# A conv-gated FFN on one core: seven half-sized products in place of eight in the up projection, activations through DRAM, and the down projection in one accumulation

## The chip, the cores and the metric

The kernel runs on one core of a Trainium2 chip. The metric is the device time of one execution in microseconds (us), and the number given for a kernel is the median of its runs.

## The reference, cut to what matters

Two transformer-like blocks follow one another on 1024 tokens of 1024 features in float32: a short-convolution layer, a stick-breaking attention layer, and a second block with two kinds of attention and a feed-forward part. The change is in the feed-forward part, which is the last thing that is computed before the final norm:

```python
D_MODEL = 1024; SEQ = 1024; D_FF = 2816; CONV_WIDTH = 3

def _conv_ffn(h, w_up, conv_w, conv_b, w_down):
    u = h @ w_up                                   # [1024, 1024] @ [1024, 5632]
    a, g = jnp.split(u, 2, axis=-1)
    s = a.shape[1]
    ap = jnp.pad(a, ((0, 0), (CONV_WIDTH - 1, 0), (0, 0)))
    a = ap[:, 0:s] * conv_w[0] + ap[:, 1:s + 1] * conv_w[1] + ap[:, 2:s + 2] * conv_w[2] + conv_b
    return (jax.nn.gelu(a, approximate=False) * g) @ w_down   # [1024, 2816] @ [2816, 1024]
...
        h2 = _rmsnorm(x, norm2_g[l]) * (1.0 + scale2) + shift2
        x = x + gate2 * _conv_ffn(h2, w_up[l], conv_w[l], conv_b[l], w_down[l])
    return _rmsnorm(x, final_g)
```

## The kernel before, in words

Activations lie feature-major: 128 features on the partitions, 512 tokens (a half) along the free dimension. Every float32 product is made of three matmuls on a rounded type: the weights are split into a high part `wh` (a cast by ScalarE) and a low part `wl` (a subtraction by VectorE), the activations likewise into the two halves of a tile `act`. For each 128x128 block of weights the function `proj` issues wh x high, wh x low and wl x high into one PSUM bank; a job with eight such blocks (eight k-tiles) is 24 matmuls of 512 columns. All matmuls of this kind are called `pj` in the profile.

Weights come as pieces of up to four k-tiles (256 KB). The list `stream` holds them in the order of use; `advance` issues the loads (SyncE's queue, SP) five pieces ahead of the use, the high parts three ahead and the low parts two ahead (eight, five and four in the last projection).

The instructions of all engines are put in order when the program is built. The class `Sched` keeps a rough clock for every engine. The projections drive; everything else is a side task, a generator that yields what it waits for and goes on once the clock of TensorE has passed that time. `until` runs side tasks until a condition holds. So the order on each engine is fixed, and on the chip an engine waits only where its next instruction isn't ready.

There are 34 large tiles (4 KB a partition) and 32 small ones (2 KB). `room` makes a side task wait until a large tile can be had.

The feed-forward part takes the 22 blocks of 128 features of `a` and of `g` in three groups (8, 7 and 7). For each group, `ups` makes the jobs `job_up` (all eight k-tiles, then the convolution, gelu and the gate in `post`, and the split of the result into an `act` tile that stays on chip), and `downs` makes the eight jobs of the down projection over the k-tiles of that group; its partial result is added to the residual and goes to DRAM (`x5_d`) and back. The first group runs half by half; in the rest (`lagged`) the second half of the tokens follows two jobs behind the first, with the same weights. The last group's second half runs in two passes of 256 tokens, so that the final norm of one can be done beside the other.

Before that, in block 2, the jobs `c1` make queries, keys and values of the second half of the tokens, attention of the second half runs as side tasks, `br` and `wo` are the output projections of each half, and `g1` are gate projections. `consume_ffn` makes the feed-forward input `h2` of the second half, `h2_side` that of the first.

Of the kernel before, what the change touches and what calls it, by code (L numbers as in the profile page):

```python
# [16 lines left out]
D = 1024  # L17
# [4 lines left out]
NF = DFF // 128  # L22
EPS = 1e-6
# [24 lines left out]
N_C = 2  # jobs before the first output of block 2  # L48
N_U = 2  # jobs kept for after the second branches
# [170 lines left out]
class Engine:  # L220
    """An engine whose instructions are noted by the scheduler."""
# [24 lines left out]
def tile_net(tc, *aps, **kw):  # L246
    """Emitted once into a context of its own, to learn when each tile is used last, then into tc."""
# [9 lines left out]
def tile_body(  # L257
# [95 lines left out]
    def advance(n):  # L353
        """Pieces up to n are about to be used."""
# [10 lines left out]
    def split_pieces(n):  # L365
        """Side task: the parts of the first pieces, as they arrive."""
# [79 lines left out]
    def proj_tok(pieces, name, half, b, ps, c0):  # L446
        """[128 tokens, 256 features] of token block b of a half: activations stationary."""
# [14 lines left out]
    def lagged(jobs, lag):  # L462
        """Jobs (pieces, fn(half, pieces)): the second half of the tokens runs lag jobs behind."""
# [12 lines left out]
    def staged(jobs, half):  # L476
        """All the jobs at once, each in a bank of its own, in stages of two k-tiles."""
# [46 lines left out]
    def load_vectors(items, tag, q):  # L524
        """1-D vectors as columns [128, n / 128]."""
# [37 lines left out]
    def gemv_add(acc, wt, sc, k, first=False):  # L563
        """The rows of k-tile k, weighed, summed over k-tiles only."""
# [5 lines left out]
    def sums(acc, turned):  # L570
        """Sums over the partitions of a [128, 512] tile, as columns: element p of each 128 on partition p."""
# [40 lines left out]
    def rstd_of(v, width):  # L612
        """v ** -0.5 on a narrow tile: square root, reciprocal, a Newton step."""
# [15 lines left out]
    def spread(r):  # L629
        """[128 tokens, 4] -> [128, 512], the same on every partition."""  # L630
# [11 lines left out]
    def rstd_rows(acc, n):  # L642
        """Squares, still to be summed over the partitions -> r of 512 tokens on every partition."""
# [8 lines left out]
    def norm_apply(xt, rb, gs, sh, key):  # L652
        """(x * gs) * r + sh, split."""
# [24 lines left out]
    x5_d = [scratch(f"x5_d{i}", [8, 128, S]) for i in range(2)]  # L678
# [8 lines left out]
    # ======================= block 1, convolution layer =======================  # L687
# [63 lines left out]
    def res_jobs(w, name, gate, x_dram, out_dram, done=None, extra_g=None, k0=0, nk=8, squares=True, pairs=False):  # L751
# [37 lines left out]
        def job(j):  # L789
# [8 lines left out]
            return chunk(w, j * 128, nk=nk, k0=k0), fn  # L798
# [5 lines left out]
    def norm_side(consume):  # L804
        """After the residual of a half: r for its tokens, then consume(r)."""
# [6 lines left out]
    def each(xs, gen, gap=1.25):  # L812
        """A task per tile, started one after the other."""
# [1019 lines left out]
```

## Time and profile before

| what | value |
|---|---|
| median of 3 runs | 2653.97 us (2653.41 to 2655.66) |
| span of the profiled execution, first to last instruction | 2650.7 us |
| time of the profiled execution itself | not listed beside its span; the median of the runs is 3.3 us above the span |
| TensorE busy | 2613.5 us (99%) |
| VectorE, ScalarE, GpSimd busy | 1635.7 us (62%), 1154.7 us (44%), 171.4 us (6%) |
| moved by DMA | 430.66 MB, 162 GB/s over the span |

The busy time of TensorE (PE) counts from an instruction's start to its modelled end, and those overlap; the distance from start to start is what a matmul costs. PEld are weight loads, which overlap the matmuls. DVE is VectorE, ACT ScalarE, POOL GpSimd; L241 and L242 are the lines of the helper through which all instructions are issued, so groups are told apart by the names of their tiles.

### The profile page before, as it was taken

The numbers are of one execution on the slowest core, as the hardware profiler recorded it, in microseconds if no ns is written. First come the engines' busy times: TensorE is split into PE (matmuls) and PEld (weight loads), VectorE is DVE, ScalarE is ACT, GpSimd is POOL, SyncE is SP. The second block draws the span as 40 slices with busy tenths as digits, with TensorE's granted clock in tenths as the row PEclk, the third lists the DMA queues.
The fourth block names the chain that finished last, engine by engine and source line by source line (L and its number), as shares of the span: only waits on it lengthen the run. The fifth ranks groups of instructions, "written<-read, shape, count | busy, mean of one in ns | idle before, by whom it ended". The sixth has DMA issues, their size and how long they took to land.

```text
span 2650.7 us, 38451 instructions
## 1 busy us (share of the span) xinstructions
PE 2613.5 (99%) x13919; PEld 2152.3 (81%) x13919; DVE 1635.7 (62%) x2984; ACT 1154.7 (44%) x2330; POOL 171.4 (6%) x308
## 2 busy tenths in 40 slices
PE   7999999999999999999999999999999999999998
PEld 6888888889877777788878887888888888888888
DVE  7866667775376789887756546657645533323346
ACT  5311113442355667686744335547433322212223
POOL 0000000111100001000001011000000000000000
PEclk9999999999999999999999999999999999999999
DMA  8855557576666654565656565762445341142136
GB/s 281 262 159 158 164 176 229 187 242 215 195 191 182 195 145 144 169 162 147 192 161 207 162 195 167 212 176 72 147 151 167 103 135 48 52 140 76 46 100 188
DMA packets 477190, 430.66 MB, mean 162 GB/s; under 512 B 25662, under 2 KB 385352, under 8 KB 477000
## 3 DMA queue, kind: packets, MB, share of 16 engines
q1 hardware_dynamic: 451252, 347.90, 45.2%
q0 software_dynamic: 23392, 76.09, 7.9%
q10 hardware_dynamic: 2356, 4.21, 0.4%
q8 instruction: 110, 1.80, 0.3%
q14 instruction: 80, 0.66, 0.1%
HBM read 346.83 MB, written 81.26 MB: 162 GB/s over the span
## 4 chain that ended last, share of the span: by engine, by line
PE 93%; DVE 4%; ACT 1%; issue 1%; DMA 1%; SPq 0%; DVEq 0%; ACTq 0%
PE pj L241 75%; PE pv L241 5%; PE z L241 4%; PE o L241 4%; PE tr L242 3%; DVE om L242 2%; DVE be L242 1%; PE sm L242 1%; DVE wl L242 0%; DMA wr<-in_b_w_qz_dram 0%; DVE act L242 0%; PE rb L242 0%; DMA mw<-in_a_mod_w_dram 0%; PE yt L242 0%; ACT om L242 0%
## 5 line engine op out<-in xcount | busy, mean ns | idle before, releaser
L241 PE MATMUL pj<-act,wh 128*128 128x512 f32 (+1 forms) x6000 | 1874.1, 394 | 5.4 <-DVE act L242 3.3
L241 PEld LDWEIGHTS pj<-act,wh 128*128 128x128 f32 x6000 | 1099.9, 189 | 235.2 <-DVE act L242 3.9
L241 PE MATMUL pj<-act,wl 128*128 128x512 f32 (+1 forms) x3000 | 1170.8, 390 | 0.0
L241 PEld LDWEIGHTS pj<-act,wl 128*128 128x128 f32 x3000 | 564.7, 188 | 127.3
L242 DVE TENSOR_TENSOR wl<-wr,wh 128x512 fp32r<-128x512 f32 (+1 forms) x670 | 444.4, 680 | 121.9 <-ACT wh L242 120.6
L242 ACT CAST wh<-wr 128x512 fp32r<-128x512 f32 (+1 forms) x670 | 394.4, 616 | 150.0 <-PE pj L241 81.7
L242 ACT COPY aT<-tr 128x512 f32<-128x512 f32 (+3 forms) x272 | 129.2, 505 | 143.9 <-PE tr L242 137.6
L241 PE MATMUL z<-kd,qs 128*128 128x256 f32 (+2 forms) x704 | 165.1, 349 | 0.0
L242 DVE SCALAR_TENSOR_TENSOR xn<-pj,mod,xo 128x512 f32<-128x512 f32 (+1 forms) x72 | 49.7, 691 | 170.8 <-PE pj L241 170.8
L242 DVE SCALAR_TENSOR_TENSOR fa<-pj,vecc,fa 128x511 f32<-128x511 f32 x88 | 65.9, 749 | 136.6 <-ACT fa L242 135.1
L242 DVE SCALAR_TENSOR_TENSOR acc<-mw,silu_c,acc 128x512 f32<-128x512 f32 x196 | 146.8, 749 | 3.4 <-DMA mw<-in_a_mod_w_dram 0.3
L241 PE MATMUL pv<-wh,act 128*128 128x256 f32 x768 | 141.0, 283 | 0.0
L241 PEld LDWEIGHTS z<-kd,qs 128*128 128x128 f32 x704 | 114.1, 190 | 16.9 <-issue 6.3
L242 DVE TENSOR_TENSOR_SCAN om<-om 128x640 f32<-128x640 f32 (+3 forms) x64 | 120.7, 1886 | 5.9 <-ACT om L242 5.9
L241 PEld LDWEIGHTS pv<-wh,act 128*128 128x128 f32 x768 | 119.4, 189 | 0.1
L242 POOL DMA_DIRECT2D x_d<-xn x80 | 43.5, 544 | 1162.2 <-DVE xn L242 1161.9
L241 PEld LDWEIGHTS o<-aT,vp 128*64 128x64 f32 (+1 forms) x1440 | 99.5, 150 | 19.4 <-issue 12.3
L241 PE MATMUL o<-aT,vp 128*64 128x128 f32 (+1 forms) x1440 | 115.2, 282 | 0.0
L242 ACT ACTIVATE fa<-pj,vecb,vecc 128x512 f32<-128x512 f32 x44 | 34.3, 779 | 175.3 <-PE pj L241 175.2
L241 PE MATMUL pv<-wl,act 128*128 128x256 f32 x384 | 108.0, 281 | 0.3 <-DVE wl L242 0.3
L242 DVE TENSOR_TENSOR fa<-fa,pj 128x512 f32<-128x512 f32 x44 | 30.2, 687 | 107.8 <-PE pj L241 107.8
L242 ACT ACTIVATE p<-p,t 128x256 f32<-128x256 f32 (+7 forms) x128 | 81.3, 636 | 25.5 <-DVE t L242 25.4
(187 smaller groups left out, 2163.8 us busy)
## 6 DMA issues: line engine op xcount, KB each, us to landing
wr<-in_w_in_dram SPq DMA_DIRECT2D x136, 256.0 KB, 3.2
wr<-in_w_up_dram SPq DMA_DIRECT2D x120, 256.0 KB, 2.9
mw<-in_w_ada_dram SPq DMA_DIRECT2D x96, 256.0 KB, 3.5
wr<-in_a_w_in_dram SPq DMA_DIRECT2D x80, 256.0 KB, 3.5
x_d<-xn POOLq DMA_DIRECT2D x80, 256.0 KB, 3.2
xo<-x_d SPq DMA_DIRECT2D x72, 256.0 KB, 3.0
wr<-in_b_w_qz_dram SPq DMA_DIRECT2D x64, 256.0 KB, 4.1
qs<-q_d SPq DMA_DIRECT2D x64, 256.0 KB, 6.6
```

What stands on the lines that cost most here:

```text
L241: return f(out, *value, **kw)
L242: return f(out=out, **kw)
```

## The change

The up projection of 1024 tokens x 1024 features x 5632 columns is cut in half along all three: tokens into halves 0 and 1, features (k) into 0 to 3 and 4 to 7, columns of `a` and of `g` into 11 blocks each. Eight half-sized products become seven, with sums of the operands made beforehand and sums of the products made afterwards:

- `weight_sums`: four sums of half-sized weight blocks for `a` and for `g`, made in DRAM by 128 DMAs on GpSimd's queue, 64 rows of 1408 floats each (64 plain copies and 64 that add to what lies there), 9 us of the planner's clock apart from 110 us on.
- `combined`: from the second half's norm, the four operand sums T1 to T4 and the second half's own k-tiles 4 to 7, as 20 `act` tiles, in four tasks 6 us apart.
- `up_first`: two products for 11 blocks of `a` and of `g` of half 0. They give the first 11 blocks of half 0; the first product is also copied out (`s1`) and goes to DRAM.
- `up_rest`: five products for each of 22 blocks, in a staggered order `first`, `last` of the block before, `middle`. VectorE adds to a PSUM bank between products, and ScalarE copies two intermediate sums (`u`, `v`) per block.
- The results (`act_d`) go to DRAM and come back as `act` tiles (`act_side`, `act_one`).
- The down projection is one accumulation over all 22 k-tiles in the order `DOWN`, three passes: half 0, and half 1 in two passes of 256 tokens. The rounds through `x5_d` are gone.
- `c1` runs before the first output projection `br` and not partly after it, and the up jobs beside `br` and `wo` are now `up_first` of 4, 1 and 6 blocks.

Comments and docstrings are gone as well. The core of the diff:

```diff
+M_BR = 4
+M_WO = 5
+T_SUM = 110.0
+E_SUM = 9.0
+R_SUM = 64
...
-    def res_jobs(w, name, gate, x_dram, out_dram, done=None, extra_g=None, k0=0, nk=8, squares=True, pairs=False):
...
-            return chunk(w, j * 128, nk=nk, k0=k0), fn
+            return [Piece(w, k, n, j * 128, 128) for k, n in ks], fn
...
-        each(xs, lambda j, x: norm_apply(x, rb, GS["2"][:, j:j + 1], V["sh2"][:, j:j + 1], ("h2", j, half)))
+        for i in range(4):
+            sch.spawn(combined(i, rb, xs[i], xs[4 + i]), i * 6.0)
+    def combined(i, rb, x0, x1):
+        stt = vec.scalar_tensor_tensor
+        h = []
+        for k, x in ((i, x0), (4 + i, x1)):
+            stt(out=x, in0=x, scalar=GS["2"][:, k:k + 1], in1=rb, op0=ALU.mult, op1=ALU.mult)
+            yield x
+            act(out=x, in_=x, func=ACTF.Identity, bias=V["sh2"][:, k:k + 1])
+            h.append(x)
+        a0, a1 = act_of(("h2", i, 0)), act_of(("h2", 4 + i, 0))
+        yield h
+        t1, t2 = sml(name="T1"), sml(name="T2")
+        vec.tensor_tensor(out=t1, in0=f32(a0[:, 0, :]), in1=h[0], op=ALU.subtract)
+        vec.tensor_tensor(out=t1, in0=t1, in1=f32(a0[:, 1, :]), op=ALU.add)
+        stt(out=t2, in0=h[1], scalar=-1.0, in1=t1, op0=ALU.mult, op1=ALU.subtract)
+        yield t2
+        yield from split_to(("T", 2, i), t2)
+        vec.tensor_tensor(out=h[0], in0=h[1], in1=h[0], op=ALU.subtract)
+        yield h[0]
+        yield from split_to(("T", 3, i), h[0])
+        yield from split_to(("T", 1, i), t1)
+        stt(out=t2, in0=t2, scalar=-1.0, in1=f32(a1[:, 0, :]), op0=ALU.mult, op1=ALU.subtract)
+        vec.tensor_tensor(out=t2, in0=t2, in1=f32(a1[:, 1, :]), op=ALU.subtract)
+        yield t2
+        yield from split_to(("T", 4, i), t2)
+        yield from split_to(("h2", 4 + i, 1), h[1])
+        flags.add(("T", i))
...
+    def weight_sums():
+        def W(k, f, n):
+            return w_up[512 * k:512 * k + 512, n * DFF + f * HF:n * DFF + (f + 1) * HF]
+        while sch.t < T_SUM:
+            yield 2.0
+        for n in range(2):
+            g = [sg_d[i][n] for i in range(4)]
+            for to, of, op in ((0, W(0, 1, n), None), (2, W(0, 0, n), None), (0, W(1, 1, n), ALU.add),
+                               (2, W(0, 1, n), ALU.add), (1, W(0, 0, n), None), (3, W(1, 0, n), None),
+                               (1, g[0], ALU.add), (3, g[1], ALU.add)):
+                for r in range(0, 512, R_SUM):
+                    kw = {"accum_op": op, "max_dma_last_dim": HF * 4} if op else {}
+                    pol.dma_start(out=g[to][r:r + R_SUM], in_=of[r:r + R_SUM], **kw)
+                    yield E_SUM
...
+            store(act_d[f, :, hs(half)], t)
+            flags.add(("act", f, half))
...
+    def product(ps, pc, keys, start=False):
+        use(pc)
+        for i, key in enumerate(keys):
+            a = act_of(key)
+            sch.turn(sch.when((a, pc.h, pc.l)))
+            first = start and i == 0
+            mm(ps, lhsT=pc.h[:, i, :], rhs=a[:, 0, :], start=first, stop=False, skip_group_check=not start)
+            mm(ps, lhsT=pc.h[:, i, :], rhs=a[:, 1, :], start=False, stop=False, skip_group_check=not start)
+            mm(ps, lhsT=pc.l[:, i, :], rhs=a[:, 0, :], start=False, stop=i == 3, skip_group_check=not start)
...
+    def up_first(ms):
+        todo = [(m, [(w, block(m, w, 0, 0), block(m, w, 1, 0)) for w in "ag"]) for m in ms]
+        for _, two in todo:
+            stream.extend([two[0][1], two[1][1], two[0][2], two[1][2]])
+        def run():
+            for m, two in todo:
+                pss = []
+                for w, p0, _ in two:
+                    sch.turn(sch.bank_time())
+                    ps = bank("pj")
+                    product(ps, p0, h2_of(0, 0), True)
+                    store(s1_d["ag".index(w), m], copied(ps, "s1"))
+                    pss.append(ps)
+                for ps, (w, _, p1) in zip(pss, two):
+                    product(ps, p1, h2_of(1, 0))
+                    then(up_out(m, w, 0, ps, False))
+        return run
+    def up_rest():
+        todo = [(m, w, {2: summed(m, w, 2), 3: summed(m, w, 3), 1: summed(m, w, 1), 5: block(m, w, 1, 1),
+                        4: summed(m, w, 4)}) for m in range(NM) for w in "ag"]
+        for n, (_, _, p) in enumerate(todo):
+            stream.append(p[2])
+            if n:
+                stream.extend([todo[n - 1][2][5], todo[n - 1][2][4]])
+            stream.extend([p[3], p[1]])
+        stream.extend([p[5], p[4]])
+        def T(n):
+            return [("T", n, i) for i in range(4)]
...
+        def out_11(f, w, ps, v):
+            t = sml(name="y11")
+            vec.tensor_tensor(out=t, in0=ps, in1=v, op=ALU.add)
+            sch.keep(ps)
+            then(up_out(f, w, 1, t, True))
+        def run():
+            got = {n: fetch(n) for n in range(2)}
+            st = {}
+            def first(n):
+                m, w, p = todo[n]
+                sch.turn(sch.bank_time())
+                b2 = bank("pj")
+                product(b2, p[2], T(2), True)
+                s1 = got.pop(n)
+                vec.tensor_tensor(out=b2, in0=b2, in1=s1, op=ALU.add)
+                sch.keep(b2)
+                st[n] = [b2, copied(b2, "u")]
+                if n + 2 < len(todo):
+                    got[n + 2] = fetch(n + 2)
+            def middle(n):
+                m, w, p = todo[n]
+                b2 = st[n][0]
+                product(b2, p[3], T(3))
+                v = copied(b2, "v")
+                sch.turn(sch.bank_time())
+                b4 = bank("pj")
+                product(b4, p[1], T(1), True)
+                out_11(m + NM, w, b4, v)
+                st[n].append(b4)
+            def last(n):
+                m, w, p = todo[n]
+                b2, u, b4 = st.pop(n)
+                product(b2, p[5], T(4))
+                then(up_out(m + NM, w, 0, b2, True))
+                product(b4, p[4], h2_of(1, 1))
+                vec.tensor_tensor(out=b4, in0=b4, in1=u, op=ALU.add)
+                sch.keep(b4)
+                then(up_out(m, w, 1, b4, False))
+            for n in range(len(todo)):
+                first(n)
+                if n:
+                    last(n - 1)
+                middle(n)
+            for k in [("T", n, i) for n in (1, 2, 3) for i in range(4)]:
+                del A[k]
+                free()
+            last(len(todo) - 1)
+            for k in [("T", 4, i) for i in range(4)] + h2_of(1, 1):
+                del A[k]
+                free()
+        return run
+    DOWN = [(0, 4), (NM, 4), (4, 4), (NM + 4, 4), (8, 3), (NM + 8, 3)]
+    def act_side(half):
+        fs = [f + i for f, n in DOWN for i in range(n)]
+        for k, f in enumerate(fs):
+            yield from wait(("act", f, half))
+            yield from room(1)
+            sch.spawn(act_one(k, f, half))
+            yield 0.7
+    def act_one(k, f, half):
+        t = sml(name="al")
+        syn.dma_start(out=t, in_=act_d[f, :, hs(half)])
+        yield t
+        yield from split_to(("act", k, half), t)
...
-    run_br0, run_c1a, run_wo0, run_c1 = alone(br, 0), alone(c1[:N_C], 1), alone(wo, 0), alone(c1[N_C:], 1)
+    run_c1, run_br0, run_wo0 = alone(jobs_c1(), 1), alone(br, 0), alone(wo, 0)
...
-    run_up0 = alone(up0[:16 - N_U], 0)
+    run_up0 = up_first(range(M_BR))
     run_br1 = alone(again(br), 1)
-    run_up0b = alone(up0[16 - N_U:], 0)
+    run_up0b = up_first(range(M_BR, M_WO))
     run_wo1 = alone(again(wo), 1)
-    run_down0 = alone(downs(0), 0)
-    run_up1 = alone(ups(0), 1)
-    run_down1 = alone(downs(0), 1)
-    run_ffn = lagged(ups(1) + downs(1) + ups(2), 2)
-    last = downs(2, True)
+    run_up0c = up_first(range(M_WO, NM))
+    run_up1 = up_rest()
+    last = res_jobs(w_down_2[0], "act", "gt2", x4_d, None, final, ks=DOWN, squares=False)
...
+        run_c1()
         sch.until(lambda: ("attn2", 0) in flags)
         run_br0()
-        run_c1a()
         run_wo0()
-        run_c1()
         sch.spawn(h2_side())
         run_g1()
         run_up0()
         run_br1()
         run_up0b()
         run_wo1()
-        run_down0()
+        run_up0c()
+        sch.spawn(h2_end())
+        sch.spawn(act_side(0))
         run_up1()
-        run_down1()
-        run_ffn()
+        sch.spawn(act_side(1), 60.0)
```

## Rows read from the trace of the kernel before

**Rows 1.** the head of the profile page and its busy times by engine
```profile
span 2650.7 us, 38451 instructions
...
PE 2613.5 (99%) x13919; PEld 2152.3 (81%) x13919; DVE 1635.7 (62%) x2984; ACT 1154.7 (44%) x2330; POOL 171.4 (6%) x308
```
**Rows 2.** the chain that ended last, its shares by line
```profile
PE pj L241 75%; PE pv L241 5%; PE z L241 4%; PE o L241 4%; PE tr L242 3%; DVE om L242 2%; DVE be L242 1%; PE sm L242 1%; DVE wl L242 0%; DMA wr<-in_b_w_qz_dram 0%; DVE act L242 0%; PE rb L242 0%; DMA mw<-in_a_mod_w_dram 0%; PE yt L242 0%; A
```
**Rows 3.** by stage: busy us and count by engine, then clock, DMA share, GB/s
```profile
800.00:1000.00 200.00, 192.96 (x1263) 151.85 (x1261) 152.43 (x183) 127.67 (x290) 17.07 (x26) 0.99 0.59 169
...
2200.00:2400.00 200.00, 200.00 (x865) 162.14 (x864) 68.67 (x118) 44.20 (x75) 7.56 (x14) 1.00 0.27 85
```
**Rows 4.** projection matmuls by shape: out<-in, shape, count, busy us, mean ns
```profile
L241 PE MATMUL pj<-act,wh 128*128 128x512 f32 x5776 | 1833.8, 399 | 5.4 <-DVE act L242 3.3 <-ACT act L242 2.1
...
L241 PE MATMUL pj<-act,wh 128*128 128x256 f32 x224 | 40.3, 283 | 0.0
```
**Rows 5.** the same chain in order of time: start us, us, instructions
```profile
1999.96 578.21 PE pj L241 x2493
```
**Rows 6.** timeline of PE in the last pass: start us, us, instructions
```profile
2633.59 0.28 PE L241 MATMUL pj<-act,wl 128*128 128x256 f32 x1
...
2641.03 0.28 PE L241 MATMUL pj<-act,wl 128*128 128x256 f32 x1
```
**Rows 7.** the timeline near 1350, and the 25 us window around it
```profile
1353.39 0.50 PE L241 MATMUL pj<-act,wh 128*128 128x512 f32 x1 [1.77 <-ACT act L242]
...
1350.00:1375.00 25.00, 23.00 (x93) 18.04 (x91) 13.20 (x21) 11.66 (x22) 0.54 (x1) 0.93 0.42 130
```
**Rows 8.** vector and scalar groups by shape: count, busy us, mean ns
```profile
L242 DVE TENSOR_TENSOR wl<-wr,wh 128x512 fp32r<-128x512 f32 x638 | 428.9, 686 | 121.2 <-ACT wh L242 119.9 <-DMA wr<-in_b_w_out_dram 0.4 <-issue 0.3
L242 ACT CAST wh<-wr 128x512 fp32r<-128x512 f32 x638 | 380.9, 621 | 119.8 <-PE pj L241 59.6 <-DMA wr<-in_b_w_qz_dram 15.1 <-DMA wr<-in_a_w_in_dram 12.0
...
L242 ACT ACTIVATE fa<-pj,vecb,vecc 128x512 f32<-128x512 f32 x44 | 34.3, 779 | 175.3 <-PE pj L241 175.2
```
**Rows 9.** timeline of VectorE around the end of the second output projection
```profile
1977.51 1.28 DVE L242 TENSOR_TENSOR wl<-wr,wh 128x512 fp32r<-128x512 f32 x2
...
1987.95 0.75 DVE L242 SCALAR_TENSOR_TENSOR xn<-pj,mod,xo 128x512 f32<-128x512 f32 x1 [3.00 <-PE pj L241]
...
2000.83 0.75 DVE L242 SCALAR_TENSOR_TENSOR nt<-xn,gs,rb 128x512 f32<-128x512 f32 x1
...
2002.09 1.41 DVE L242 SCALAR_TENSOR_TENSOR nt<-xn,gs,rb 128x512 f32<-128x512 f32 x2
```
**Rows 10.** a stage of up and down projections, columns as in rows 3
```profile
2100.00:2200.00 100.00, 100.00 (x433) 81.03 (x432) 40.45 (x68) 27.85 (x47) 4.32 (x8) 1.00 0.40 119
```
**Rows 11.** DMA issues by line: count, KB each, median us to landing
```profile
wr<-in_w_up_dram SPq DMA_DIRECT2D x120, 256.0 KB, 2.9
...
x_d<-xn POOLq DMA_DIRECT2D x80, 256.0 KB, 3.2
xo<-x_d SPq DMA_DIRECT2D x72, 256.0 KB, 3.0
```
**Rows 12.** timeline of VectorE between block 1's last residual and block 2's norm
```profile
1400.27 0.75 DVE L242 SCALAR_TENSOR_TENSOR xn<-pj,mod_b,xo 128x512 f32<-128x512 f32 x1 [2.24 <-PE pj L241]
...
1437.20 0.75 DVE L242 SCALAR_TENSOR_TENSOR act<-nt,mod,act 128x512 fp32r<-128x512 f32 x1
```
**Rows 13.** score matmuls z of the second half, first and last window
```profile
1575.00:1600.00 25.00, 2.61 (x16) 2.10 (x16) 3.55 (x8) 0.00 (x0) 0.00 (x0) 1.00 0.59 170
...
1850.00:1875.00 25.00, 4.18 (x16) 2.93 (x16) 5.49 (x8) 0.00 (x0) 0.00 (x0) 1.00 0.25 74
```
**Rows 14.** DMA queues: packets, MB, share of 16 engines' span
```profile
q1 hardware_dynamic: 451252, 347.90, 45.2%
q0 software_dynamic: 23392, 76.09, 7.9%
```
**Rows 15.** busy DMA beside projections, 25 us, columns as in rows 3
```profile
1425.00:1450.00 25.00, 25.00 (x110) 20.34 (x109) 18.97 (x30) 11.17 (x20) 4.44 (x9) 1.00 0.93 303
```

More of the change, by code (lines that the diff above doesn't have):

```diff
@@ L22 @@
 NF = DFF // 128
+HF = DFF // 2
+NM = NF // 2
 EPS = 1e-6
@@ L47 @@
 N_G = 7
-N_C = 2
-N_U = 2
+M_BR = 4
[3 more added lines that the diff above has]
+R_SUM = 64
 class Sched:
@@ L677, in tile_body @@
     x4_d = scratch("x4_d", [8, 128, S])
-    x5_d = [scratch(f"x5_d{i}", [8, 128, S]) for i in range(2)]
+    act_d = scratch("act_d", [NF, 128, S])
+    s1_d = scratch("s1_d", [2, NM, 128, HT])
+    sg_d = [[scratch(f"sg_d{i}{w}", [512, HF]) for w in "ag"] for i in range(4)]
     def store(dst, src):
@@ L1370, in consume_ffn @@
             return
-        each(xs, lambda j, x: norm_apply(x, rb, GS["2"][:, j:j + 1], V["sh2"][:, j:j + 1], ("h2", j, half)))
+        for i in range(4):
[26 more added lines that the diff above has]
+        flags.add(("T", i))
     def h2_side():
+        while "f" not in RB:
+            yield 1.0
         for j in range(NJ):
@@ L1377, in h2_side, with h2_end @@
         del RB["f"]
+    def h2_end():
+        for i in range(4):
+            yield from wait(("T", i))
+        drop("h2", 0)
+    w_up = w_up_2[0]
+    def weight_sums():
[12 more added lines that the diff above has]
+                    yield E_SUM
@@ L1379, in tile_body @@
     fhalo = const.tile([128, NF, 2], F32, name="fhalo")
     st_f = {}
-    def job_up(f, which, name, k):
-        c0 = f * 128 + (DFF if which == "g" else 0)
-        def post(ps, half):
-            if which == "a":
-                w = V["f_conv"]
-                w0, w1, w2 = (w[:, NF * i + f:NF * i + f + 1] for i in range(3))
-                t = sml(name="fa")
-                act(out=t, in_=ps, func=ACTF.Identity, scale=w2, bias=V["f_cb"][:, f:f + 1])
-                sch.keep(ps)
-                yield t
-                stt = vec.scalar_tensor_tensor
-                stt(out=t[:, 1:HT], in0=ps[:, 0:HT - 1], scalar=w1, in1=t[:, 1:HT], op0=ALU.mult, op1=ALU.add)
-                stt(out=t[:, 2:HT], in0=ps[:, 0:HT - 2], scalar=w0, in1=t[:, 2:HT], op0=ALU.mult, op1=ALU.add)
-                if half == 0:
-                    vec.tensor_copy(out=fhalo[:, f, :], in_=ps[:, HT - 2:HT])
-                else:
-                    hl = fhalo[:, f, :]
-                    stt(out=t[:, 0:1], in0=hl[:, 1:2], scalar=w1, in1=t[:, 0:1], op0=ALU.mult, op1=ALU.add)
-                    stt(out=t[:, 0:2], in0=hl, scalar=w0, in1=t[:, 0:2], op0=ALU.mult, op1=ALU.add)
-                yield t
-                act(out=t, in_=t, func=ACTF.Gelu)
-                st_f[f, half] = t
-            else:
-                while (f, half) not in st_f:
-                    yield 0.3
-                t = st_f.pop((f, half))
-                vec.tensor_tensor(out=t, in0=t, in1=ps, op=ALU.mult)
-                yield t
-                yield from split_to((name, k, half), t)
-        def fn(half, pieces):
-            ps = proj(pieces, "h2", half)
-            if f == NF - 1 and which == "g":
-                drop("h2", half)
-            then(post(ps, half))
-        return chunk(w_up_2[0], c0), fn
@@ new lines, in up_out @@
+    def up_out(f, which, half, src, minus):
+        if which == "a":
+            w = V["f_conv_n" if minus else "f_conv"]
+            w0, w1, w2 = (w[:, NF * i + f:NF * i + f + 1] for i in range(3))
+            t = sml(name="fa")
+            act(out=t, in_=src, func=ACTF.Identity, scale=w2, bias=V["f_cb"][:, f:f + 1])
+            hold(src)
+            yield t
+            stt = vec.scalar_tensor_tensor
+            stt(out=t[:, 1:HT], in0=src[:, 0:HT - 1], scalar=w1, in1=t[:, 1:HT], op0=ALU.mult, op1=ALU.add)
+            stt(out=t[:, 2:HT], in0=src[:, 0:HT - 2], scalar=w0, in1=t[:, 2:HT], op0=ALU.mult, op1=ALU.add)
+            if half == 0:
+                vec.tensor_copy(out=fhalo[:, f, :], in_=src[:, HT - 2:HT])
+                flags.add(("halo", f))
+            else:
+                yield from wait(("halo", f))
+                hl = fhalo[:, f, :]
+                stt(out=t[:, 0:1], in0=hl[:, 1:2], scalar=w1, in1=t[:, 0:1], op0=ALU.mult, op1=ALU.add)
+                stt(out=t[:, 0:2], in0=hl, scalar=w0, in1=t[:, 0:2], op0=ALU.mult, op1=ALU.add)
+            yield t
+            act(out=t, in_=t, func=ACTF.Gelu)
+            st_f[f, half] = t
+        else:
+            yield from has(st_f, (f, half))
+            t = st_f.pop((f, half))
+            if minus:
+                vec.scalar_tensor_tensor(out=t, in0=src, scalar=-1.0, in1=t, op0=ALU.mult, op1=ALU.mult)
+            else:
+                vec.tensor_tensor(out=t, in0=t, in1=src, op=ALU.mult)
+            yield t
+            store(act_d[f, :, hs(half)], t)
+            flags.add(("act", f, half))
@@ new lines, in hold @@
+    def hold(src):
+        if src.space == bass.MemoryType.PSUM:
+            sch.keep(src)
+    def product(ps, pc, keys, start=False):
[7 more added lines that the diff above has]
+            mm(ps, lhsT=pc.l[:, i, :], rhs=a[:, 0, :], start=False, stop=i == 3, skip_group_check=not start)
@@ new lines, in block, with summed, h2_of, copied @@
+    def block(m, which, k, f):
+        return Piece(w_up, 4 * k, 4, (DFF if which == "g" else 0) + f * HF + m * 128, 128)
+    def summed(m, which, n):
+        return Piece(sg_d[n - 1]["ag".index(which)], 0, 4, m * 128, 128)
+    def h2_of(k, half):
+        return [("h2", 4 * k + i, half) for i in range(4)]
+    def copied(ps, name):
+        t = sml(name=name)
+        sca.copy(out=t, in_=ps)
+        sch.keep(ps)
+        return t
+    def up_first(ms):
[15 more added lines that the diff above has]
+        return run
@@ L1518, in tile_body @@
     c1 = jobs_c1()
-    run_br0, run_c1a, run_wo0, run_c1 = alone(br, 0), alone(c1[:N_C], 1), alone(wo, 0), alone(c1[N_C:], 1)
+    run_c1, run_br0, run_wo0 = alone(jobs_c1(), 1), alone(br, 0), alone(wo, 0)
     run_g1 = alone(jobs_g(0) + jobs_g(1, True), 1)
-    xs_d = [x4_d] + x5_d + [None]
-    def ups(g):
-        f0, nf = ((0, 8), (8, 7), (15, 7))[g]
-        return [job_up(f0 + k, which, f"act{g}", k) for k in range(nf) for which in "ag"]
-    def downs(g, last=False):
-        f0, nf = ((0, 8), (8, 7), (15, 7))[g]
-        return res_jobs(w_down_2[0], f"act{g}", "gt2", xs_d[g], xs_d[g + 1],
-                        final if last else None, k0=f0, nk=nf, squares=False)
-    up0 = ups(0)
-    run_up0 = alone(up0[:16 - N_U], 0)
+    run_up0 = up_first(range(M_BR))
     run_br1 = alone(again(br), 1)
-    run_up0b = alone(up0[16 - N_U:], 0)
+    run_up0b = up_first(range(M_BR, M_WO))
     run_wo1 = alone(again(wo), 1)
-    run_down0 = alone(downs(0), 0)
-    run_up1 = alone(ups(0), 1)
-    run_down1 = alone(downs(0), 1)
-    run_ffn = lagged(ups(1) + downs(1) + ups(2), 2)
-    last = downs(2, True)
+    run_up0c = up_first(range(M_WO, NM))
+    run_up1 = up_rest()
+    last = res_jobs(w_down_2[0], "act", "gt2", x4_d, None, final, ks=DOWN, squares=False)
     run_last = [alone(last, 0)] + [alone(again(last), (1, c0, 256)) for c0 in (0, 256)]
@@ L1685, in mods_2 @@
             act(out=sc2, in_=V["c2"], func=ACTF.Silu)
+            while "f_conv" not in V:
+                yield 1.0
+            V["f_conv_n"] = const.tile([128, 3 * NF], F32, name="f_conv_n")
+            vec.tensor_scalar(out=V["f_conv_n"], in0=V["f_conv"], scalar1=-1.0, scalar2=None, op0=ALU.mult)
             yield from gemv_side(w_ada_2[0], 0, 6 * D, sc2, mod_2, V["b_ada"], EVERY)
@@ L1750, in tile_body @@
         sch.spawn(mods_1())
+        sch.spawn(weight_sums())
         for run in run_a:
```

8 lines of the change are left out of this document (added).

## Prediction

> **What bounds the kernel now.** I read the head of the page first: TensorE is busy for 2613.5 of 2650.7 us, every other engine far less [rows 1]. A busy time can hide queueing, so next the chain that ended last: 75% of it is projection matmuls (`pj`), and the vector and scalar work in it are a few per cent [rows 2]. Then the stages: only where attention is densest does TensorE show gaps (192.96 of 200 us); in the up projection it shows none, while VectorE is busy a third and ScalarE a fifth of the time [rows 3]. So there a matmul left out is time left out, as long as nothing else becomes late.
>
> The price of a matmul is its distance from the next, not the mean of some 399 ns that the groups list [rows 4]: over the last long stretch of the chain, 2493 matmuls of 512 columns took 578.21 us, 231.9 ns each [rows 5]. In the passes of 256 columns, 63 matmuls lie between two starts 7.44 us apart, 118.1 ns each [rows 6].
>
> A rule of the Trainium skill gives another price (TensorE: Matmul & The Clock Gate, the section on why 56 ns and not 53.3): columns / 2.4 GHz + 2.5 ns, 215.7 ns for 512. The stretch above ran at a granted clock of 1.00 and shows 231.9; the measurement decides. By the page the whole sum below would come out at some 2611.
>
> **What is removed and added on TensorE.** Before, the up projection has 44 blocks x 2 halves x 24 = 2112 matmuls. After, `up_first` has 22 x 24 = 528 and `up_rest` 22 x 60 = 1320, together 1848. 264 fewer x 231.9 ns = **-61.2 us**. The down projection keeps 1056 matmuls' worth, but the second half's two passes of 256 tokens now hold all 22 k-tiles and not 7: 360 matmuls of 512 become 720 of 256, 720 x 118.1 - 360 x 231.9 ns = **+1.5 us**. With every other cost hidden the span would be 2650.7 - 59.7 = 2591.0.
>
> **What a wait costs.** Near 1350 us TensorE waits about 2.0 us for two activation tiles; the 25 us around it hold 93 matmuls and not 25 / 0.2319 = 108, with a mean granted clock of 0.93: 3.4 us lost for 2.0 waited, as the clock fell to its lower level (1.2 of 2.4 GHz) after the gap [rows 7]. I take 1.7 us for each us of a wait of that size.
>
> **Vector and scalar work.** A subtraction or addition on 512 columns lasts 686 ns, a cast 621, a scaled one on ScalarE 779 [rows 8]; in a row they come closer, two `wl` in 1.28 us and two scalar_tensor_tensor (stt) in 1.41, so 0.60 and 0.66 us apart [rows 9].
>
> *`up_first`.* For each of 22 blocks ScalarE must copy the first product out before the second is added to the same bank. The other letter's product, 12 matmuls or 2.8 us, lies between; the copy is 0.62 us, so 2 us are left for what stands ahead of it in ScalarE's queue (casts of 0.62, a gelu that waits for VectorE). From nothing to 22 x 0.62 = 13.6 us if no copy is covered; I take 2, since the two engines are less than half busy there.
>
> *`combined`.* Each of the four tasks has 9 additions and 4 stt on VectorE, 9 x 0.60 + 4 x 0.66 = 8.0 us, 32 in all. Cover is the third `up_first`: 6 x 48 matmuls = 66.8 us. The norm ahead of it takes 13 us from the last residual of the second output projection to the first scaled tile [rows 9], which leaves 54 us; in them `up_first` itself wants 4 `wl`, 2 stt and one product per 11.1 us, about 4.4 us, or 21. 32 + 21 = 53: VectorE is full just as `up_rest` begins. Low parts of weights, made only two pieces (5.6 us) ahead, stand in the same queue behind these tasks, and TensorE behind them. T4 and the h2 tiles are wanted 11 us later than T2. Bounds: nothing, and 15 us (the last two tasks' 16 us wholly late). I take 4.
>
> *`up_rest`.* For a pair of blocks (27.8 us of TensorE) VectorE has 10 `wl`, 6 additions for the products, 3 gates, 1.3 low parts of results and 6 stt: 20.3 x 0.60 + 6 x 0.66 + 1 for the halo columns = 17 us, 61%, against 40% in the stage before [rows 10]. ScalarE: 15.3 casts and copies and 3 x (0.78 + 0.63) = 13.7 us, 49%. Neither is full. What is new is that TensorE waits for them inside a block: after product 2, VectorE adds in the bank and ScalarE copies it before product 3. Two products, 24 matmuls or 5.6 us, lie between; the chain is 0.7 + 0.6 us plus queues. Bounds: nothing, and 22 x 0.7 = 15 us. I take 3.
>
> *The results through DRAM.* Store and load land in 3.2 and 3.0 us [rows 11]; with gate, store, load and split the last result of half 0 is ready about 10 us after its product, and is used as the 22nd k-tile, 2.8 + 14.6 us after: hidden. A load of such a tile waits on SP for its store to land, and the loads of weights are queued behind it; they are issued five pieces (14 us) ahead, which covers some 5 us of that. At most 14 of the 22 tiles fit beside the 20 operand tiles (34 in all), the other 8 load while the 14 are used (9.7 us): hidden. The change of halves is tighter. Half 0's 22 tiles, the final norm's 4 and its gain leave 7 places, so 15 tiles of half 1 are loaded only as half 0's are given back, 0.7 us apart, 10.5 us and the 3 us of a load, while the first job of the pass uses a tile every 0.35 us. In program order these loads stand behind the last job of half 0, but SP and ScalarE run some pieces ahead of TensorE, so I count part of the lag of about 8 us: **4**, between nothing and 8 x 1.7 = 14.
>
> *Moved work.* `c1` now needs the second half's norm one job series after the last residual (7 gate jobs, 39 us, and not 83). That norm took 1400.3 to 1438.0, 37.7 us [rows 12]: just in time, 0 to 3 us, I take 0. Attention of the second half ran from 1575 to 1875 [rows 13] beside 68 us of `c1`, 89 of `g1` and 78 of up jobs, 235 us. Now it has 68 + 89 and 44.5 each of `br`, `wo` and up jobs, 290 us: hidden. If that cover failed, the wait for the attention's end would show before `br` of half 1. The order of the change loads and splits 82 more weight pieces (34 up, 48 down); the splits are in the sums above, and in the passes of 256 a piece is used in 1.4 us against 0.60 us on VectorE.
>
> *`weight_sums`.* 128 DMAs of 0.36 MB between 110 and some 1270 us, on POOL's queue, where stores wait behind them for the time of an issue. I take 0 (see the rivals).
>
> **Sum.** -61.2 + 1.5 + 2 + 4 + 3 + 4 = -46.7; span 2604.0. The profile lists no time of its execution beside the span, and the runs' median lies 3.3 us above it, so **2607 us**. 0.2% (5 us) is about what runs of this kernel can tell from no change.
>
> **Rivals.**
> *All is hidden.* No new wait: 2591.0 + 3.3 = 2594. For it: TensorE shows no gap in any stage of up projections now. Against it: `combined` fills VectorE, and the change of halves lacks room. Chance 0.15.
> *VectorE and ScalarE set the pace of the up projection.* All upper bounds at once except one: 13.6 + 15 + 15 + 4 = 47.6 in place of 13, 2642; half of the addition, 2624, is its likelier part. For it: both engines' queues are in order, and a gelu that waits for VectorE holds up a copy that TensorE waits for. Against it: 61% and 49%. Chance 0.17.
> *The sums in DRAM hold up loads.* 347.9 MB took 45.2% of 2650.7 us on the main queue, 3.4 us of all engines per MB [rows 14], so a DMA of 0.36 MB is 1.2 us, one that adds perhaps twice that: 14 to 28% every 9 us, on top of 59% [rows 3]. Yet a window at 93% left TensorE at 25.00 of 25 us [rows 15]. Priced at four waits like that near 1350, 14 us: 2621. Chance 0.05. The Trainium skill (DMA: Bandwidth & Descriptors, the section that issuing engines are not separate DMA queues) has transfers of all issuing engines on the same 16 DMA engines, which speaks for this rival; the trace's 93% window speaks against its price.
> *Slower.* The chain between product 2 and product 3 is late in every block by one wait of 2.0 us, with its 3.4 us: 22 x 3.4 = 75 in place of 3, 2679. It decides from (46.7 + 3) / 22 = 2.3 us per block on, that is if VectorE's and ScalarE's queues hold more than some 6 us when product 2 ends. The queues' shares make that unlikely. Chance 0.04.
>
> **Chances and range.** The forecast's own case (waits of 5 to 25 us, 2599 to 2619) has the rest, 0.59. Low end: all hidden, 2593. High end: the first half of the second rival and the third, 2631; beyond it lie the slower case and that rival's upper part. Faster 0.94, same 0.02, slower 0.04.
>
> **What would show it.** 9096 `pj` matmuls, 1056 of them of 256 columns; 232 and 118 ns apart. Waits of TensorE for VectorE or ScalarE at three places: the first blocks of `up_rest`, steadily inside it, and at the first pass of 256. The forecast is wrong if TensorE has gaps between product 2 and 3 of most blocks, if there are waits for weight loads before 1270 us, or if attention of the second half ends late.

## The result, and the profile after

The changed kernel takes **2668.2 us** (median of 4 runs, 2666.6 to 2669.0) beside 2653.7 us for the kernel before on the same chip: a ratio of 1.0052, 95% interval 1.0038 to 1.0066. It is slower by 0.5%, where 2607 us was forecast. The profiled execution has a span of 2666.9 us.

The head of the page, the busy times and the two main DMA queues (name, packets, MB, share of 16 engines), which answer to [rows 1, 14]:

```profile
span 2666.9 us, 39606 instructions
PE 2570.2 (96%) x14015; PEld 2126.0 (80%) x14015; DVE 1724.5 (65%) x3137; ACT 1232.9 (46%) x2492; POOL 276.0 (10%) x469
...
q1 hardware_dynamic: 497252, 377.01, 48.6%
q0 software_dynamic: 36272, 130.88, 16.2%
```

TensorE is busy 43 us less than before, and the span is 16 us longer: some 60 us of idle time have come in. GpSimd's DMA queue (q0) has twice its share of before.

The matmuls of the projections, by tile (count, ns least/median/most, first and last start, forms), answer to [rows 4]:

```profile
L246 PE MATMUL pj<-act,wh x6064: 274/394/796, 61.9 to 2657.4; 128*128 128x512 f32 x173, 128*128 128x256 f32 x23
L246 PE MATMUL pj<-act,wl x3032: 276/393/628, 65.4 to 2657.5; 128*128 128x512 f32 x168, 128*128 128x256 f32 x22
```

6064 + 3032 = 9096, as forecast. So the work did go away. By the prediction's own prices the span without any new wait would be 2591.0; it is 2666.9, so 75.9 us are new waits and not 13. Windows by stage (busy time and count of each engine, granted clock, DMA share, GB/s) tell where they are; the profile's DMA shares can come out a little above 1:

```profile
core 0: us, PE busy (x) PEld busy (x) DVE busy (x) ACT busy (x) POOL busy (x), PEclk, DMA share, GB/s
0.00:66.00 66.00, 13.54 (x50) 10.57 (x51) 17.13 (x35) 15.83 (x27) 22.31 (x42) 1.00 1.01 287
66.00:700.00 634.00, 633.99 (x3128) 529.28 (x3128) 441.28 (x734) 194.52 (x337) 52.77 (x87) 1.00 0.70 218
...
925.00:950.00 25.00, 19.61 (x109) 16.02 (x107) 17.94 (x21) 15.24 (x37) 5.89 (x10) 0.86 1.04 299
...
2200.00:2300.00 100.00, 100.00 (x432) 80.81 (x431) 66.40 (x117) 46.53 (x83) 4.86 (x9) 1.00 0.57 172
...
2510.00:2545.00 35.00, 27.37 (x160) 23.92 (x159) 22.57 (x44) 17.68 (x39) 4.60 (x8) 0.80 0.79 259
```

The same first window of the kernel before, and 45 us of it by themselves:

```profile
0.00:66.00 66.00, 51.18 (x237) 41.48 (x238) 52.59 (x99) 38.49 (x68) 4.15 (x13) 0.97 0.89 281
5.00:50.00 45.00, 34.60 (x152) 28.08 (x153) 37.65 (x68) 23.96 (x42) 0.14 (x1) 0.96 1.10 347
```

So the DMA engines were full from 5 to 50 us before the change too (1.10); the 0.89 is a mean over that and a quieter end.

**The start** is the largest: 13.54 us of TensorE in 66, against 51.18. What each engine waits for there (us in total, times, longest):

```profile
DVE acc L247 <- DMA mw<-in_a_mod_w_dram: 38.9, 5, 11.6
ACT wh L247 <- DMA wr<-in_a_w_in_dram: 30.5, 3, 27.9
...
PE sm L246 <- DVE acc L247: 20.2, 1, 20.2
PE rb L247 <- DVE t L247: 15.3, 1, 15.3
```

VectorE and ScalarE wait for loads of weights (`mw` the modulation's, `wr` a projection's), and TensorE for them. In the kernel before, TensorE's same two waits (`sm` and `rb` are small sums and copies for the modulation and the norm) are short:

```profile
PE rb L242 <- DVE t L242: 3.4, 1, 3.4
...
PE sm L241 <- DVE acc L242: 1.1, 1, 1.1
```

GpSimd's timeline says what else uses the DMA engines at that time (start, us, instruction, count, idle before):

```profile
5.15 1.53 POOL L247 DMA_DIRECT2D sg_d0a<-in_w_up_dram  x3
8.35 2.52 POOL L247 DMA_DIRECT2D sg_d0a<-in_w_up_dram  x5 [1.67 <-DMA rows<-in_kv_mod_b_dram]
10.95 0.50 POOL L247 DMA_DIRECT2D sg_d2a<-in_w_up_dram  x1
...
22.06 0.83 POOL L247 DMA_DIRECT2D sg_d0a<-in_w_up_dram  x1 [0.63 <-DMA sg_d2a<-in_w_up_dram]
...
40.62 0.78 POOL L247 DMA_DIRECT2D sg_d2a<-in_w_up_dram  x1 [1.14 <-DMA sg_d0a<-in_w_up_dram]
447.48 0.82 POOL L247 DMA_DIRECT2D x_d<-xn  x1 [406.07 <-DVE xn L247]
448.28 0.82 POOL L247 DMA_DIRECT2D sg_d2a<-in_w_up_dram  x1
```

29 of the 128 weight sums run from 5 to 41 us, 105 us before the time written in the code, and the 30th at 448 us, right behind the first store that waits for data. The constant `T_SUM = 110` is a time of the planner's clock: it fixes where the sums stand in GpSimd's queue, and in that queue nothing that waits stood ahead of them.

**Smaller losses.** At the end of the second half's attention, and around the start of `up_rest` (TensorE's timeline):

```profile
1909.84 1.09 PE L247 MATMUL rb<-ident,t 128*128 128x128 f32 x4 [3.96 <-DVE t L247]
...
2065.29 0.50 PE L246 MATMUL pj<-act,wl 128*128 128x512 f32 x1 [1.08 <-DVE wl L247]
2085.99 0.72 PE L246 MATMUL pj<-act,wh 128*128 128x512 f32 x2 [1.41 <-ACT u L247]
```

**The change of halves.** The first pass of 256 tokens begins at 2515.36 us. Windows of the `pj` matmuls alone:

```profile
core 0: us, PE busy (x) PEld busy (x) DVE busy (x), PEclk, DMA share, GB/s
2515.00:2520.00 5.00, 4.33 (x31) 3.65 (x29) 0.00 (x0) 1.00 0.66 182
2520.00:2525.00 5.00, 2.49 (x9) 1.49 (x9) 0.00 (x0) 0.87 0.91 306
2525.00:2530.00 5.00, 2.73 (x11) 2.33 (x11) 0.00 (x0) 0.50 1.08 368
2530.00:2535.00 5.00, 2.74 (x12) 2.44 (x12) 0.00 (x0) 0.50 1.08 386
2535.00:2540.00 5.00, 4.88 (x34) 4.58 (x33) 0.00 (x0) 0.77 0.96 316
2540.00:2545.00 5.00, 5.00 (x45) 5.00 (x44) 0.00 (x0) 1.00 0.72 214
```

97 matmuls in 25 us, where 118.1 ns each makes 212: (212 - 97) x 0.1181 = 13.6 us lost. Matmuls that start 0.4 us apart count as half busy; the column to read is the count.

### The profile page after: what moved, and what is told of

The parts are those of the page before. It is cut to its first block, busy times and chain, and to the rows that moved or that the text cites. A ratio compares the mean times of both kernels' runs of the same rounds, so it can differ in the third digit from the quotient of the medians.

```text
span 2666.9 us, 39606 instructions
## 1 busy us (share of the span) xinstructions
PE 2570.2 (96%) x14015; PEld 2126.0 (80%) x14015; DVE 1724.5 (65%) x3137; ACT 1232.9 (46%) x2492; POOL 276.0 (10%) x469
## 4 chain that ended last, share of the span: by engine, by line
PE 89%; DVE 5%; DMA 2%; SPq 2%; ACT 2%; issue 1%; DVEq 0%; ACTq 0%
PE pj L246 71%; PE pv L246 5%; PE o L246 4%; PE z L246 4%; PE tr L247 3%; SPq L247 2%; DVE om L247 2%; DVE be L247 1%; DVE wl L247 1%; PE sm L247 1%; DVE act L247 0%; DMA wr<-in_w_in_dram 0%; DMA wr<-in_b_w_out_dram 0%; DMA wr<-in_b_w_qz_dram 0%; DMA wr<-in_a_w_in_dram 0%
## 5 line engine op out<-in xcount | busy, mean ns | idle before, releaser
L246 PE MATMUL pj<-act,wh 128*128 128x512 f32 (+1 forms) x6064 | 1837.5, 386 | 21.1 <-ACT act L247 11.6
L246 PE MATMUL pj<-act,wl 128*128 128x512 f32 (+1 forms) x3032 | 1158.6, 382 | 1.4 <-DVE wl L247 1.4
L247 DVE TENSOR_TENSOR wl<-wr,wh 128x512 fp32r<-128x512 f32 (+1 forms) x752 | 493.5, 676 | 145.4 <-ACT wh L247 144.1
L247 ACT CAST wh<-wr 128x512 fp32r<-128x512 f32 (+1 forms) x752 | 444.3, 615 | 197.6 <-PE pj L246 81.7
L246 PE MATMUL z<-kd,qs 128*128 128x512 f32 (+2 forms) x704 | 166.3, 352 | 0.0
L247 DVE SCALAR_TENSOR_TENSOR xn<-pj,mod,xo 128x512 f32<-128x512 f32 (+1 forms) x40 | 25.7, 643 | 158.6 <-PE pj L246 158.6
L247 POOL DMA_DIRECT2D x_d<-xn x48 | 26.4, 550 | 653.8 <-DVE xn L247 653.6
L247 ACT ACTIVATE sq<-xn 128x512 f32<-128x512 f32 x48 | 30.5, 636 | 110.2 <-DVE xn L247 105.1
L247 DVE TENSOR_REDUCE t<-sm 128x4 f32<-128x512 f32 x40 | 27.6, 690 | 81.1 <-PE sm L247 81.1
L247 ACT COPY u<-pj 128x512 f32<-128x512 f32 x38 | 22.3, 587 | 124.4 <-PE pj L246 71.1
```

What stands on the lines that cost most here:

```text
L246: return f(out, *value, **kw)
L247: return f(out=out, **kw)
```

## The experiments

Theory: the sums cost the start, and the change of halves the second loss, by tiles that come free too late. Rival for the first: the new order of work, or the loads of the up projection through DRAM, cost what the start seems to. Rival for the second: the results' way through DRAM is itself too slow. Ratios are to the kernel before, run on the same chip.

**e1: no sums at all.**

```diff
-        return Piece(sg_d[n - 1]["ag".index(which)], 0, 4, m * 128, 128)
+        return block(m, which, n % 2, n // 2 % 2)
...
-        sch.spawn(weight_sums())
```

> The changed kernel without the 128 DMAs of the sums; the four products that use summed weights read plain blocks of w_up in their place, so the result is not the reference's, while every other transfer and instruction stays. Theory (the sums run at the very start and beside the first attention, since nothing on POOL's queue holds them back): the first projection matmul back from 61.9 to about 27 us, no loss beside the first attention, 2668 - 40 - 10 = 2618 us. Rival (the start is late for another reason, such as the order of the loads): the first matmul stays near 62 us and the time near 2668.

Measured: 2618.96 us, ratio 0.9873 [0.9859, 0.9888]. The gate tiles `gt`, made at the end of the first half's attention, come at 1290.0 us, where they came at 1339.9 in the changed kernel:

```profile
L247 ACT ACTIVATE gt<-pj x32: 574/598/605, 1290.0 to 1796.3; 128x512 f32<-128x512 f32 x32
```

50 us of the 75.9 are the sums', all of it ahead of 1340 us: 40.3 at the start (the first `u`, a tile of the first layer, comes at 105.8 us, and at 65.5 before), the rest beside the first half's attention. There the 25 us from 925 on (above) hold waits of TensorE of 3.43 and 1.92 us at a DMA share of 1.04. The same work lies 40 us earlier in e1: from 885 to 910 us it has one wait of 2.00 us, 21.55 us of TensorE and a DMA share of 0.61. Both traces hold the same 14015 instructions of TensorE in the same order. Matched one by one, the changed kernel is 40.0 us behind e1 at 475 us, 49.1 at 1075, and 50.0 from 1325 us to the change of halves.

**e2: the sums held back.** Emitted from 410 us of the planner's clock, they stand behind the stores that begin there.

```diff
-T_SUM = 110.0
+T_SUM = 410.0
```

> The changed kernel with the sums begun at 410 us of the planner's clock and not at 110, so that in program order the first stands behind GpSimd's first store that waits for data. Theory (only the place in POOL's queue decides): first projection matmul at about 27 us, 40 us gained, 2628 us, with the first attention as slow as in the changed kernel or slower. Rival (the sums cost the same wherever they run, as their transfers share the engines): the 40 us turn up again between 410 and 1600 us, and the time stays near 2668.

Measured: 2627.3 us, ratio 0.9902 [0.9887, 0.9917]. The first `pj` matmul is back at 23.9 us (61.9 in the changed kernel, 23.3 before). One constant turns the loss into a gain. It lies 8.3 us above e1: that much the sums still cost beside later work.

**e3: the sums alone.** The kernel before, with the sums made and used by nothing.

```diff
+        sch.spawn(weight_sums())
```

> The kernel before with the sums added at the same place and not used by anything. Theory: they alone cost 40 us at the start and about 10 beside the first attention, 2654 + 50 = 2704 us. Rival (the cost comes only together with the other parts of the change): 2654 to 2660 us.

Measured: 2703.1 us, ratio 1.0189 [1.0172, 1.0206]: some 50 us for 128 DMAs that nobody reads. So no other part of the change is needed for the loss. Its first window:

```profile
0.00:66.00 66.00, 13.38 (x50) 10.40 (x51) 16.93 (x35) 15.82 (x27) 22.51 (x42) 1.00 1.01 289
```

**e10: half as many sums ahead of the first waiting store.**

```diff
-                    yield E_SUM
+                    yield 2 * E_SUM if done <= 16 else E_SUM
```

> The changed kernel as it is, but with its first 16 sums emitted 18 us apart in place of 9, so that 16 or 17 in place of 29 lie ahead of the first store that holds GpSimd's queue; the other sums follow 9 us apart as before. Theory (the start waits for DMA engines in proportion to the sums in them): the loss at the start falls from 40 us to about 22, so 2650 us. Rival (a fixed wait, such as one load caught behind the first sums or a late constant): the loss stays near 40 us and the time above 2662 us.

Measured: 2646.9 us, ratio 0.9973 [0.9963, 0.9984]. GpSimd's timeline:

```profile
5.16 1.53 POOL L247 DMA_DIRECT2D sg_d0a<-in_w_up_dram  x3
...
19.14 0.50 POOL L247 DMA_DIRECT2D sg_d2a<-in_w_up_dram  x1 [0.60 <-DMA sg_d0a<-in_w_up_dram]
422.51 0.56 POOL L247 DMA_DIRECT2D x_d<-xn  x1 [402.88 <-DVE xn L247]
...
427.82 0.51 POOL L247 DMA_DIRECT2D sg_d2a<-in_w_up_dram  x1
```

15 sums, all plain copies, lie at the start now, and the first `u` comes at 80.8 us, 15.3 late: 1.0 us a copy. The 29 of the changed kernel, 16 copies and 13 that add, made it 40.3 late; the 14 more cost 25.0, 1.8 us each. The loss grows with the number of sums, as the theory says and a fixed wait would not. It is smaller than the 22 us expected, which counted all sums alike. That the kind of DMA makes the difference, and not its place, no run tests by itself, but the changed kernel's windows point to it: from 10 to 25 us, when the sums under way are mostly copies, the full engines move 359 GB/s; from 30 to 45 us, when they are mostly adding ones, 221:

```profile
10.00:25.00 15.00, 1.32 (x7) 0.91 (x5) 2.31 (x5) 3.18 (x7) 7.04 (x13) 1.00 1.03 359
30.00:45.00 15.00, 0.00 (x0) 0.00 (x0) 1.50 (x2) 0.00 (x0) 5.29 (x7) 1.00 1.05 221
```

The kernel's time falls by 21.3 us and not by the 25.0 that the start gives: some 4 us are lost again by 750 us, 3 of them in one wait of TensorE for a `wh` at 724 us.

**e4: tiles given back as they are used.** In the last job of half 0's down projection each `act` tile is given back at its last matmul, and not all at the job's end.

```diff
                 sch.turn(sch.when((a, pc.h, pc.l)))
+                if drop_as_used:
+                    del A[name, k, h]
+                    free()
...
-                if j == 7 and c0 + n == HT:
+                if j == 7 and c0 + n == HT and name != "act":
                     drop(name, h)
```

> The changed kernel, but the last job of half 0 of the down projection gives back each activation tile as it uses it and not all 22 at its end, so the loads of half 1 can be issued up to 15 us earlier. Theory (the 13 us lost in the first pass of 256 columns come from tiles asked for too late): the half-rate stretch near 2525 us goes, 2668 - 13 = 2655 us. Rival (the loads, casts and low parts of 15 tiles can't be made faster than TensorE uses them, DMA and VectorE being full there): at most 3 us gained, 2665 us.

Measured: 2653.8 us, ratio 1.0004 [0.9994, 1.0013], 14.4 us less than the changed kernel. The windows around the change of halves, all engines:

```profile
core 0: us, PE busy (x) PEld busy (x) DVE busy (x) ACT busy (x) POOL busy (x), PEclk, DMA share, GB/s
2500.00:2525.00 25.00, 25.00 (x161) 22.59 (x160) 20.54 (x40) 19.85 (x46) 1.32 (x3) 1.00 0.90 282
2525.00:2550.00 25.00, 25.00 (x215) 25.00 (x214) 15.06 (x29) 10.21 (x20) 3.00 (x6) 1.00 0.84 258
```

No gap and no lower clock, though the same tiles take the same way through DRAM and the DMA share is 0.90. The way is not too slow; the loads began too late. In the changed kernel's trace SyncE issues 12 of the 15 late loads of `act` tiles between 2516.3 and 2524.8 us, in two runs of six, all behind the last matmul of the job, which starts at 2515.1 us; the other three go out between 2502.9 and 2513.2.

**e5: both together** (`T_SUM = 410.0` and the edit of e4).

> The changed kernel with both single edits together: the weight sums emitted from 410 us of the planner's clock on, and each activation tile of the last down job of half 0 given back as soon as its last matmul is recorded. If the losses at the start and at the change of halves are two separate waits, the gains add: 2627 less the 13 to 14 us that the early freeing gave, 2613 us. Rival: part of the two gains is one and the same, and it stays above 2620 us.

Measured: 2615.8 us, ratio 0.9856 [0.9841, 0.9872]. 40.9 + 14.4 would make 2612.9; the gains add but for 3 us. Matched matmul by matmul, the change of halves itself gives 13.7 us in e4's trace and 13.6 in e5's. These are two separate losses.

**e6: a fifth `up_first` block beside the second attention.**

```diff
-M_BR = 4
-M_WO = 5
+M_BR = 5
+M_WO = 6
```

> As the kernel with held sums and early freeing, but with five in place of four of the up projection's first-half blocks beside the second half's attention. Theory: the 4 to 5 us of PE idle time at the end of the second attention goes, because PE then has another block of matmuls to fill it: 2609 us. Rival: the combined stage has one block less to cover its VectorE work (55.7 us of matmuls in place of 66.8) and gives it back: 2613 us or more.

Measured: 2615.0 us, ratio 0.9856 [0.9840, 0.9872]: no change from e5, the rival's case. Two windows of e5 and then the same two of e6:

```profile
1850.00:1900.00 50.00, 46.04 (x218) 37.96 (x218) 28.42 (x51) 21.39 (x36) 2.17 (x4) 0.97 0.55 170
...
2000.00:2060.00 60.00, 57.24 (x245) 45.40 (x244) 52.57 (x90) 36.57 (x65) 6.51 (x12) 1.00 0.63 190
```

```profile
1850.00:1900.00 50.00, 50.00 (x245) 41.37 (x244) 29.19 (x54) 24.15 (x40) 3.78 (x7) 1.00 0.62 194
...
2000.00:2060.00 60.00, 53.73 (x221) 41.86 (x220) 52.90 (x88) 35.10 (x63) 5.42 (x10) 0.97 0.52 165
```

The wait at the attention's end is gone (46.04 to 50.00), and `combined`, which has lost a block of cover, takes as much back (57.24 to 53.73). `up_first` is the cover of both, and there is not enough for both.

**e7 and e8: the sums behind the first attention** (`T_SUM = 1215.0`, `E_SUM = 5.5`, the edit of e4; e8 with e6's constants too). In both the last sums stand in the queue behind loads of the blocks that they complete, so part of the products of `up_rest` read unfinished sums, and the result is not the reference's; the number and size of all transfers is that of the changed kernel.

> As the kernel with held sums and early freeing, but with the sums emitted only after the first attention (from 1215 us of the planner's clock on, 5.5 us apart). Theory: the 7.5 us that the held sums still cost, about 4.5 near 900 us and 3 near 1359 us, go as well: 2606 us. Rival: the same traffic costs as much beside the second attention, and the time stays at 2613 us.

> Late sums, early freeing and five blocks beside the second attention in one kernel. Theory: the three gains add, 2601 to 2602 us, and the up projection by seven products then gives most of the 61 us of its matmuls: faster than before by 1.9%. Rival: late sums and the extra block's weight loads meet in the same stretch, and it is no faster than the better of the two, 2606 us or more.

Measured: e7 2607.2 us, ratio 0.9827 [0.9809, 0.9844]; e8 2605.8 us, 0.9819 [0.9804, 0.9835]. The fifth block gives 1.4 us and not 4 to 5, as in e6.

**e9: the same, with the sums done in time** (`E_SUM = 4.0`).

> Early freeing, and the sums emitted after the first attention, as in the kernel with late sums, but 4 us apart in place of 5.5, so that by the planner's clock the last of the 128 is emitted at 1727 us, ahead of the first loads of the summed blocks (in the kernel at 5.5 us apart the last sums came behind them, so that part of its products read unfinished sums). Theory: the sums then cost next to nothing: 2607 us, as at 5.5 us apart. Rival: they need the DMA engines more densely beside the second attention, where the weight and score loads run, and it stays at the 2615 to 2616 us of the held sums with early freeing.

Measured: 2612.3 us, ratio 0.9844 [0.9828, 0.9860], between the two. Its windows:

```profile
1375.00:1850.00 475.00, 472.06 (x2449) 390.86 (x2448) 288.26 (x672) 232.47 (x462) 106.44 (x172) 1.00 0.88 250
1850.00:1900.00 50.00, 45.92 (x214) 37.80 (x213) 30.45 (x56) 21.59 (x37) 12.48 (x16) 0.93 1.00 247
```

The sums run from 1311 to 1872 us here. From the first `gt` to the last, 506.3 us in e7, 510.6 pass, with one wait of 2.0 us for a `wh` among them: the denser traffic costs some 4 us again. e9 beats both the kernel before and the changed one, by 1.6% and 2.1%.

## Why the prediction was wrong

**The step that failed** is `weight_sums`: "128 DMAs of 0.36 MB between 110 and some 1270 us, on POOL's queue ... I take 0". They cost 50 us, which is more than the whole gain that was forecast (46.7), and alone turn the sign: without them (e1) the change gains 1.3%. Two things in it were wrong.

- *The time.* 110 us is the planner's; the prediction read it as the chip's. The planner only orders instructions on an engine; on the chip GpSimd ran on until one of them waited. Between 5 us and the first `x_d` store its queue had nothing that waits for the work on the other engines (that store starts at 407 us in the kernel before), and the 29 sums ahead of it went out from 5 us on. In e2 the same sums stand behind those stores, and the start is whole again.
- *The cover.* The prediction named a window at 93% DMA that left TensorE at 25.00 us [rows 15]. There, weights lay ready some pieces ahead. In the first 60 us nothing lies ready: TensorE's first matmuls wait for what VectorE and ScalarE make of the loads, and the DMA share was 1.10 from 5 to 50 us already before the change. Further transfers there add about their own time: 15.3 us for the 15 copies of e10, where [rows 14] priced one at 1.2 us.

The rival "the sums in DRAM hold up loads" had the mechanism and was given 0.05. Its price of a DMA, 1.2 us and perhaps twice that for one that adds, comes out near what the start shows (1.0 for a copy, 1.8 for the later ones). Its place and sum did not: four waits, 14 us. The rule of the Trainium skill named there (DMA: Bandwidth & Descriptors, the section that issuing engines are not separate DMA queues) is what these traces show: with 29 of GpSimd's transfers in the way, the work that waits for SyncE's loads came 40.3 us late. Whether the DMA engines or the DRAM behind them set that price was not separated.

**The term that was mis-sized** is the change of halves: 4 us forecast, 14 as its upper end, 13.6 by the count and 14.4 by e4. The prediction named the cause (loads stand behind the last job of half 0) and then let SyncE's lead over TensorE take most of it. For 12 of the 15 loads there is none: they wait for tiles that are all given back at the job's end. The lower clock adds its part: after the first gaps it is 0.50, 1.2 of 2.4 GHz, for 10 us.

**Right or nearly so.**
- The matmuls: 9096, of which 1056 of 256 columns, at the forecast prices; 1581 in a row took 367.28 us, 232.3 ns each, against 231.9.
- `up_rest`: 3 us forecast, 100.00 of 100 us measured (window 2200 to 2300 above, beside [rows 3]). VectorE is at 66%, near the 61% worked out. The slower rival, a wait between product 2 and 3 in every block, is not there.
- `combined`: 4 us forecast; waits of 1.08 and 1.41 us, and 202 matmuls in the 50 us from 2050 on where 216 fit: 3.2 us.
- `up_first`: 2 us forecast; TensorE is idle for 0.9 us in all from 1500 to 1909 us, and from 1910 to 2090 for 0.4 us beside the two waits of `combined`.
- `c1`: no wait to be seen where it moved to.

**Half right.** "290 us: hidden" for the second attention. Its end is 4 us late for `rb` (1909.84), in e1 too, so by the new order of work and not by the sums. e6 shows that one more block would hide it, and that this block is needed elsewhere.

40.3 + 9.7 + 13.6 + 3.2 and some 4 for the attention's end make 71 of the 75.9 us. The rest was not located. Of the three signs that the prediction named for being wrong, two came: waits for weight loads before 1270 us, and attention of the second half that ends late.

**With the two repairs**, e5 comes to 2615.8 and e9 to 2612.3 us, inside the range and 9 and 5 us above the forecast: what is left of the sums (e9 is 5 us above e7), and the attention's end.

## What to carry to other kernels

A time in a planner orders a queue and holds nothing: for each added DMA, look for the last instruction ahead of it on its engine that waits in the trace, and take that as the earliest time it runs. Transfers that are called free because they fit between others can be dear in the first tens of microseconds, where no stock of loaded weights covers a wait: here the start took 40.3 of the sums' 50 us. Where one buffer's tiles hand over to the next, ask when each is given back, not only how many there are; and a block of cover moved to one wait is taken from another.

## What was not expected of the hardware

- A copy from DRAM to DRAM of 0.36 MB on GpSimd's queue delays the start by 1.0 us (15 of them, e10), the next 14, of which 13 add, by 1.8 us each, though GpSimd issues a copy in 0.50 and an adding one in 0.78 us: the cost is in the shared transfers (DMA share 1.04 from 5 to 50 us), not on the engine that issues.
- While the tiles come in one at a time at the change of halves, 11 or 12 matmuls of 256 columns run in 5 us and the granted clock is 0.50 for 10 us; with the tiles in time (e4) the same stretch keeps 1.00.
